# The opening of a two-block transformer kernel put in a set order, worked by token halves

## The chip, the cores and the metric

The kernel runs on one core of a Trainium2 chip. Times are microseconds (us) of device time for the whole kernel, the median of the runs. The engines: TensorE (PE in the profile; its weight loads are PEld), VectorE (DVE), ScalarE (ACT), GpSimd (POOL) and SyncE (SP), which here only issues DMAs. Each works through its instructions in one fixed order and waits at the first whose inputs or buffers are not ready.

## The reference, cut to what matters

Two transformer blocks of two layers each, 512 tokens, width 1024, float32. Only the beginning is touched by the change: a layer norm without weights, a scale and a shift from a conditioning vector (adaLN), and the first columns of a projection.

```python
def first_block(x, c, w_in, ...):
    c_act = jax.nn.silu(c)
    h = layer_norm(x)                      # mean and variance over 1024 features, per token
    for l in range(DEPTH):
        ada = (c_act @ w_ada[l] + b_ada[l])[:, None, :]
        sh1, sc1, g1, sh2, sc2, g2 = jnp.split(ada, 6, axis=-1)
        u = h * (1.0 + sc1) + sh1
        y = mixer(u, w_in[l], ...)         # z = u @ w_in, then mLSTM heads, attention, gates
        h = layer_norm(DN_ALPHA * h + g1 * y, ...)
        ...
```

The second block needs `softplus(-lam)` of a vector of 512 (here `softplus_cols`), long after the opening.

## The kernel before, in words

Activations lie transposed: features on the 128 partitions, 512 tokens along the free dimension, so x is 8 tiles of 128 x 512 (`self.x`, k from 0 to 7, called inputs below). A product multiplies a 128 x 128 block of weights with such a tile. For accuracy each operand is split into a rounded high part and a remainder (`h`/`l` of an activation, `wh`/`wl` of a weight), and a product is three matmuls: wh by h, wh by l, wl by h. All weights come as one stream (`block`): SP loads chunks of 16 blocks (1 MB, two buffers), and a unit of 8 blocks is cast on ACT (`wh`, L589) and its remainder taken on VectorE (`wl`, L592) when its first block is wanted; there are 5 buffers for units, so a cast can wait until products have released one.

The opening is `setup` and the first half of `first_block`. `setup` issues the loads (SP and ACT share them): the vectors, the constants for sums, x whole, the other constants; it makes silu of c, softplus (`softplus_cols`, a Tanh and an Exp of one table set on ACT, 27 small instructions on VectorE), and scales columns of the vectors. Then the norm: `Mean.half` sums over features by matmuls with ones into a PSUM bank; `spread` copies the sums to SBUF and spreads them with one more matmul; `mean` subtracts and squares; `scale` takes the reciprocal root and corrects it in three steps (`rstd`); `plain` multiplies (five tiles on VectorE, three on GpSimd). For every input k, `ada_tile` loads four tiles of adaLN weights (1 MB in all), sums them against silu(c) on TensorE (L820), copies the sums (L824) and turns them to columns (L827, L829); the output u of input k is formed from these columns (L1360 to L1362), GpSimd scales the residual (L1364), and five products follow (L1367 to L1369): the gates and four tiles of head 0's queries and keys, in five PSUM banks.

Behind it `mlstm_gates` takes the gates' accumulator through ACT and VectorE (L884 to L905, three table loads among them and around), and TensorE meanwhile works at the values of head 0 (`proj_tokens`, L625 to L629) until it needs the transposed gates (L911). The order of all this on each engine is made by a scheduler from the program's text and its dependencies, unless `behind` ties two instructions.

Later norms already work by token halves: `mean`, `squares`, `scale` and `out` take a half (`hs`), and `proj_halves` forms the products of the first 256 tokens of several accumulators, then of the second; `residual` then rescales the tile itself. The lines the prediction uses from there are L238 (sums), L248 (spread), L347 (copy of the mean), L349, L352 (subtract, square), L855 (reciprocal root), L377 to L379 (output), L649 to L653 (products).

Of the kernel before, what the change touches and what calls it, by code (L numbers as in the profile page):

```python
# [16 lines left out]
P = 128  # L17
# [209 lines left out]
class Mean:  # L227
# [16 lines left out]
    def spread(self, tmp, hs):  # L244
        m, nc = self.m, self.m.nc
        nc.scalar.copy(tmp.f[:, hs], self.rows[:, hs])
# [31 lines left out]
class Norm:  # L278
# [3 lines left out]
    def __init__(self, m, r, kind, cols, res=None):  # L282
        self.m, self.r, self.kind, self.cols, self.res = m, r, kind, cols, res
        self.sum = None
# [4 lines left out]
    def start(self, total):  # L289
        if self.sum is None:  # L290
            self.sum = Total(self.m) if total else Mean(self.m, self.m.pso, "o")
# [47 lines left out]
    def mean(self, hs):  # L339

        m, nc, r = self.m, self.m.nc, self.r
        if self.kind != "ln":
            return
        if hs.start == 0:
            self.sq = Mean(m, m.pss, "s")
        mu = self.sum.spread(self.tmp, hs)
        nc.scalar.copy(self.y.f[:, hs], mu[:, hs])  # L347
        for k in range(KD):
            nc.vector.tensor_tensor(out=r[k].f[:, hs], in0=r[k].f[:, hs], in1=self.y.f[:, hs], op=ALU.subtract)  # L349
        self.sqs = [m.get() for _ in range(KD)]  # L350
        for k in range(KD):
# [10 lines left out]
    def scale(self, hs):  # L362
# [3 lines left out]
        if self.kind == "ln":  # L366
            var, eps = self.sq.spread(self.a, hs), LN_EPS
# [4 lines left out]
    def out(self, k, hs):  # L372
# [5 lines left out]
        nc.scalar.activation(h.r[:, hs], t, AF.Identity, bias=sh, scale=1.0)  # L378
# [10 lines left out]
    def plain(self, hs):  # L389

        self.mean(hs)
        self.squares(hs, 0)
        self.squares(hs, 1)
        self.scale(hs)
        for k in range(KD):
            eng = self.m.nc.gpsimd if k in (2, 5, 7) else self.m.nc.vector
            eng.tensor_tensor(out=self.r[k].f[:, hs], in0=self.r[k].f[:, hs], in1=self.y.f[:, hs], op=ALU.mult)
        self.done()

    def done(self):  # L400
        m = self.m
        if self.kind == "ln" and self.cols is not None:
# [121 lines left out]
class Model:  # L524
    def __init__(self, ctx, tc, ins, out, dbg=None, stop=None):
# [20 lines left out]
        self.later = []  # L546

# [29 lines left out]

    def block(self, name, l, k, c):
# [3 lines left out]
        if n % CHUNK == 0:  # L582
            self.wt = self.wtp.tile([P, CHUNK * P], F32, name="wt")
            nc.sync.dma_start(out=self.wt, in_=self.ins["ws"][n // CHUNK].rearrange("p a b -> p (a b)"))
        if n % UNIT == 0:
# [3 lines left out]
            copy = nc.scalar.copy(self.wh, src)  # L589
            if n == 0:  # L590
                self.behind(copy, self.last_rsqrt)
# [40 lines left out]
    def proj_halves(self, specs, xs, k0=0, by_input=False):  # L632
# [9 lines left out]
        blks = {}  # L642
# [35 lines left out]

    def split(self, src, pair):
# [20 lines left out]
    def setup(self):  # L700
        nc = self.nc
        self.vecs = self.cp.tile([P, NVEC], F32, name="vecs")
        nc.sync.dma_start(out=self.vecs, in_=self.ins["vecs"])
# [7 lines left out]
        nc.scalar.dma_start(out=self.consts, in_=self.ins["cst"][:, n:])  # L711
# [10 lines left out]
        nc.vector.tensor_copy(self.ident_r, self.ident)  # L722
        self.csil = self.cp.tile([P, 16], F32, name="csil")
        c = self.vec("c1", 0, 16)
        th = self.small(16, "th_c")
        nc.scalar.activation(th, c, AF.Tanh, scale=0.5)
        nc.vector.tensor_scalar(out=th, in0=th, scalar1=0.5, scalar2=0.5, op0=ALU.mult, op1=ALU.add)
        nc.vector.tensor_mul(self.csil, th, c)
        self.n2sp = self.softplus_cols()
        self.n4sp = self.cp.tile([P, 4], F32, name="n4sp")  # L730
        nc.vector.tensor_scalar(out=self.n4sp, in0=self.n2sp, scalar1=2.0, scalar2=None, op0=ALU.mult)
# [12 lines left out]
        nc.vector.tensor_scalar(out=v, in0=v, scalar1=1.0, scalar2=None, op0=ALU.add)  # L744
# [1087 lines left out]
```

## Time and profile before

| | |
|---|---|
| runs | 3477.12, 3477.94, 3479.91 us; median 3477.94 |
| the profiled execution | 3481.36 us, its span 3479.6 us |
| mean granted clock of TensorE over the span | 0.993 of full speed |
| TensorE busy | 98% of the span |
| VectorE, ScalarE, GpSimd busy | 62%, 42%, 5% |
| DMA | 395.72 MB, mean 114 GB/s |

Times in the profile count from the start of the span. A busy TensorE is not one at its peak, since matmuls are pipelined and their ends are modelled; the spacing of two starts says more than one duration. A matmul of plain float32 (sums, spreads, columns) shows as two instructions in the profile, one of the rounded operands (products) as one.

### The profile page before, as it was taken

Reading aid. Unit: us, or ns where it says so; the run is one execution under the profiler, and the core shown is the slowest. Engines: PE = TensorE matmul, PEld = TensorE weight load, DVE = VectorE, ACT = ScalarE, POOL = GpSimd, SP = SyncE. Lnnn points to the kernel's source line nnn. Section 1 sums busy time; section 2 is a strip of 40 time slices with the busy share of each in tenths; the row PEclk is TensorE's granted clock in tenths of the full one; section 3 lists DMA queues with packets and bytes.
Section 4 is the critical chain, followed back from the end, with each engine's and each line's share of the span. In section 5 each row is a group of like instructions: output and inputs, shape, how many; then the busy total and the mean of one; then the engine's idle time right before and its main releaser. Section 6 shows DMA issues by size and latency. Waiting matters only on the chain.

```text
span 3479.6 us, 45264 instructions
## 1 busy us (share of the span) xinstructions
PE 3405.2 (98%) x17783; PEld 2787.9 (80%) x17783; DVE 2159.5 (62%) x4071; ACT 1450.8 (42%) x2536; POOL 183.8 (5%) x252
## 2 busy tenths in 40 slices
PE   7999999999999999999999999989999999999999
PEld 5788777778888888877788888877688888888887
DVE  5875545648663687554534856378888555875353
ACT  4543555225222454355523422237753234753231
POOL 1110010010000011001100000001000000000000
PEclk9999999999999999999999999999999999999999
DMA  5222223634552222222222555221146432122222
GB/s 218 91 75 84 75 78 105 223 121 176 205 188 97 73 91 79 80 84 73 79 97 85 200 187 194 94 71 61 37 145 232 163 114 85 50 74 97 97 97 73
DMA packets 76117, 395.72 MB, mean 114 GB/s; under 512 B 9200, under 2 KB 10480, under 8 KB 42496
## 3 DMA queue, kind: packets, MB, share of 16 engines
q1 hardware_dynamic: 69408, 377.90, 30.5%
q0 software_dynamic: 4480, 12.69, 1.2%
q8 instruction: 140, 2.29, 0.3%
q10 hardware_dynamic: 2016, 2.25, 0.2%
q14 instruction: 73, 0.60, 0.1%
HBM read 390.60 MB, written 2.20 MB: 113 GB/s over the span
## 4 chain that ended last, share of the span: by engine, by line
PE 85%; DVE 7%; ACT 2%; DMA 2%; issue 1%; POOL 0%; DVEq 0%; ACTq 0%; POOLq 0%
PE acc L604 22%; PE acc L606 21%; PE acc L605 21%; PE acc L649 2%; PE acc L652 2%; PE acc L653 2%; DMA wada<-in_ada_dram 1%; PE o L1168 1%; PE o L1583 1%; DVE wl L592 1%; PE s L1132 1%; DVE slot L778 1%; PE acc L625 1%; PE acc L629 1%; PE acc L628 1%
## 5 line engine op out<-in xcount | busy, mean ns | idle before, releaser
L604 PE MATMUL acc<-slot,wh 128*128 128x512 f32 x3461 | 1375.7, 398 | 14.0 <-DVE slot L874 9.3
L605 PE MATMUL acc<-slot,wh 128*128 128x512 f32 x3461 | 1364.0, 394 | 0.0
L606 PE MATMUL acc<-slot,wl 128*128 128x512 f32 x3461 | 1363.3, 394 | 0.0
L589 ACT CAST wh<-wt 128x1024 fp32r<-128x1024 f32 x522 | 547.2, 1049 | 1230.0 <-PE acc L605 1021.9
L592 DVE TENSOR_TENSOR wl<-wt,wh 128x1024 fp32r<-128x1024 f32 x522 | 647.7, 1242 | 526.1 <-ACT wh L589 521.3
L604 PEld LDWEIGHTS acc<-slot,wh 128*128 128x128 f32 x3461 | 652.7, 189 | 164.2 <-ACT wh L589 13.9
L606 PEld LDWEIGHTS acc<-slot,wl 128*128 128x128 f32 x3461 | 652.1, 188 | 146.6 <-issue 4.9
L605 PEld LDWEIGHTS acc<-slot,wh 128*128 128x128 f32 x3461 | 652.9, 189 | 140.8 <-issue 5.4
L778 DVE SCALAR_TENSOR_TENSOR slot<-wada,csil,slot 128x512 f32<-128x512 f32 x308 | 232.1, 754 | 63.2 <-DMA wada<-in_ada_dram 57.6
L649 PE MATMUL acc<-slot,wh 128*128 128x256 f32 x726 | 206.9, 287 | 6.2 <-ACT slot L512 5.9
L652 PE MATMUL acc<-slot,wh 128*128 128x256 f32 x726 | 205.6, 283 | 0.0
L653 PE MATMUL acc<-slot,wl 128*128 128x256 f32 x726 | 204.3, 282 | 0.1
L680 ACT CAST slot<-slot 128x512 fp32r<-128x512 f32 x204 | 125.3, 620 | 168.9 <-DVE slot L1332 47.2
L1266 DVE SCALAR_TENSOR_TENSOR slot<-acc,ada,slot 128x512 f32<-128x512 f32 (+1 forms) x109 | 70.2, 647 | 160.8 <-PE acc L606 120.8
L874 DVE SCALAR_TENSOR_TENSOR slot<-acc,vecs,slot 128x510 f32<-128x510 f32 (+2 forms) x217 | 159.9, 746 | 7.8 <-ACT slot L869 5.2
L681 DVE TENSOR_TENSOR slot<-slot,slot 128x512 fp32r<-128x512 f32 x204 | 144.4, 714 | 30.8 <-ACT slot L680 21.3
L649 PEld LDWEIGHTS acc<-slot,wh 128*128 128x128 f32 x726 | 136.8, 189 | 13.4 <-ACT slot L512 6.5
L652 PEld LDWEIGHTS acc<-slot,wh 128*128 128x128 f32 x726 | 137.3, 189 | 2.5 <-issue 1.2
L653 PEld LDWEIGHTS acc<-slot,wl 128*128 128x128 f32 x726 | 137.4, 189 | 0.7 <-DVE wl L592 0.3
L625 PE MATMUL acc<-wh,slot 128*128 128x256 f32 x288 | 81.5, 283 | 0.0
L628 PE MATMUL acc<-wh,slot 128*128 128x256 f32 x288 | 81.4, 283 | 0.0
L629 PE MATMUL acc<-wl,slot 128*128 128x256 f32 x288 | 80.9, 281 | 0.0
(391 smaller groups left out, 3939.6 us busy)
## 6 DMA issues: line engine op xcount, KB each, us to landing
wt<-in_ws_dram SPq DMA_DIRECT2D x261, 1024.0 KB, 4.8
wada<-in_ada_dram SPq DMA_DIRECT2D x176, 512.0 KB, 4.4
slot<-in_ada_dram SPq DMA_DIRECT2D x32, 256.0 KB, 6.1
slot<-drc POOLq DMA_DIRECT2D x16, 256.0 KB, 3.5
slot<-in_bias_dram POOLq DMA_DIRECT2D x16, 256.0 KB, 3.0
slot<-dr POOLq DMA_DIRECT2D x32, 128.0 KB, 3.0
out_dram<-slot SPq DMA_DIRECT2D x8, 256.0 KB, 2.0
slot<-in_xT_dram SPq DMA_DIRECT2D x4, 256.0 KB, 5.4
```

The lines of the kernel that those rows point to most:

```text
L589: copy = nc.scalar.copy(self.wh, src)
L592: nc.vector.tensor_tensor(out=self.wl, in0=src, in1=self.wh, op=ALU.subtract)
L604: nc.tensor.matmul(acc, wh, xs[k].h.r, start=k == 0, stop=False)
L605: nc.tensor.matmul(acc, wh, xs[k].l.r, start=False, stop=False)
L606: nc.tensor.matmul(acc, wl, xs[k].h.r, start=False, stop=k == n - 1)
L649: m = nc.tensor.matmul(acc[:, hs], wh, xs[k].h.r[:, hs], start=k == 0, stop=False)
L652: nc.tensor.matmul(acc[:, hs], wh, xs[k].l.r[:, hs], start=False, stop=False)
L653: last[a] = nc.tensor.matmul(acc[:, hs], wl, xs[k].h.r[:, hs], start=False, stop=k == n - 1)
L680: copy = self.nc.scalar.copy(pair.h.r, src)
L681: self.nc.vector.tensor_tensor(out=pair.l.r, in0=src, in1=pair.h.f, op=ALU.subtract)
L778: nc.vector.scalar_tensor_tensor(out=acc.f, in0=wt[:, j, :], scalar=c, in1=acc.f, op0=ALU.mult, op1=ALU.add)
L874: nc.vector.scalar_tensor_tensor(out=out[:, lo:hi], in0=acc[:, lo + d:hi + d], scalar=w, in1=out[:, lo:hi], op0=ALU.mult, op1=ALU.add)
```

## The change

- x comes in token halves: first halves on SP and ACT, then the vectors, the first weight chunk and adaLN tile 0, then the second halves. The 16 columns of c and c_2 have a small load of their own ahead; the other constants come after the opening.
- The norm works by halves with the functions of the later norms, its first sums and its squares in one PSUM bank. `out` forms u from the centred x, the reciprocal root and the columns, so the five and three multiplications of `plain` go; the residual (alpha times the root times x) becomes eight VectorE instructions that can run later, and GpSimd's eight go.
- The products go through `proj_halves`: all five accumulators for the first 256 tokens, input by input, then again for the second. Between the products of an input stand, in this order, the next tile's sums and columns, the next output, the weights of the input after it, and a piece of the second half's norm (`other`). AdaLN tiles are loaded three ahead.
- `in_order` ties PE, DVE and ACT instructions of `first_norm` to the order of the text; instructions outside it can still be put between them by the scheduler.
- Softplus moves into `mixer`, behind the gates in the text and not ahead of the last output on ACT (`last_out`).

```diff
 class Mean:
...
+    def collect(self, tmp, hs):
+        self.m.nc.scalar.copy(tmp.f[:, hs], self.rows[:, hs])
...
 class Norm:
...
+    def means(self, hs, mu):
+        m = self.m
+        if self.sq is None:
+            self.sq = Mean(m, m.pss, "s")
+        m.nc.scalar.copy(self.y.f[:, hs], mu[:, hs])
+        self.sqs = {}
...
+    def centre(self, hs, ks):
...
-        for k in range(KD):
+        for k in ks:
             nc.vector.tensor_tensor(out=r[k].f[:, hs], in0=r[k].f[:, hs], in1=self.y.f[:, hs], op=ALU.subtract)
...
+        for k in ks:
             nc.scalar.activation(self.sqs[k].f[:, hs], r[k].f[:, hs], AF.Square)
...
-            if n == 0:
-                self.behind(copy, self.last_rsqrt)
...
+    def in_order(self):
+        traced = self.nc.cur_bb.bb.instructions
+        n = len(traced)
+        yield
+        last = {}
+        for i in list(traced[n:]):
+            if i.engine in (mybir.EngineType.PE, mybir.EngineType.DVE, mybir.EngineType.Activation):
+                if i.engine in last:
+                    self.tc.add_manual_dep(i, last[i.engine].name, mybir.DependencyInfo(
+                        mybir.DependencyClass.NoSync, mybir.DependencyReason.DATA), reason="order of the text")
+                last[i.engine] = i
...
-        for k in range(KD):
-            (nc.sync if k % 2 else nc.scalar).dma_start(out=self.x[k].f, in_=self.ins["xT"][k])
+        for hs in HALVES:
+            for k in range(KD):
+                (nc.sync if k % 2 or hs.start else nc.scalar).dma_start(out=self.x[k].f[:, hs], in_=self.ins["xT"][k][:, hs])
+            if hs.start == 0:
+                self.vecs = self.cp.tile([P, NVEC], F32, name="vecs")
+                nc.sync.dma_start(out=self.vecs, in_=self.ins["vecs"])
+                self.chunk(0)
+                self.adas = deque([self.ada_load(0)])
...
     def mixer(self, l, u):
         nc = self.nc
         gates = self.mlstm_gates(l, u)
+        if l == 0:
+            self.n2sp = self.softplus_cols()
...
-        norm = Norm(self, r, "ln", None)
-        for k in range(KD):
-            norm.half(k, slice(0, T))
-        self.behind(self.load_rsqrt(r[5].f[:, 0:1]), self.sp_exp)
-        norm.plain(slice(0, T))
...
-        for k in range(KD):
-            self.ada_tile(k)
...
+        with self.in_order():
+            norm = self.first_norm(r, A(0, 1), A(0, 0))
+        self.setup_late()
...
+    def first_norm(self, r, sc, sh):
...
+        norm = Norm(self, r, "ln", (sc, sh))
+        self.load_rsqrt(self.eps[:, 0:1])
+        norm.sq = Mean(self, self.pss, "s")
+        norm.start(False, norm.sq)
+        for k in range(KD):
+            norm.half(k, first)
+        self.setup_columns()
+        norm.mean(first)
+        weights(0)
+        norm.squares(first, 0)
+        norm.squares(first, 1)
+        norm.scale(first)
+        self.adas += [self.ada_load(1), self.ada_load(2)]
+        self.chunk(1)
+        self.ada_columns(0, self.ada_sums())
+        norm.out(0, first)
+        weights(1)
+        ahead = self.proj_halves(specs, norm.u, by_input=True, blks=blks)
...
+        def other(k):
+            if k == 1:
+                for j in range(KD):
+                    norm.half(j, second)
+                norm.sum.collect(norm.tmp, second)
+            elif k == 2:
+                norm.means(second, norm.sum.spread(norm.tmp, second, True))
+            elif k in (3, 4):
+                norm.centre(second, range(4 * k - 12, 4 * k - 8))
+            elif k == 5:
+                norm.squares(second, 0)
+                norm.squares(second, 1)
+                norm.sq.collect(norm.a, second)
+            elif k == 6:
+                norm.scale(second, True)
+
+        for k in range(KD):
+            if k + 3 < KD:
+                self.adas.append(self.ada_load(k + 3))
+            if k == 3:
+                self.chunk(2)
+            rs = self.ada_sums() if k + 1 < KD else None
+            products(range(2))
+            if rs is not None:
+                self.ada_columns(k + 1, rs)
+                norm.out(k + 1, first)
+            weights(k + 2)
+            products(range(2, 5))
+            other(k)
+        norm.out(0, second)
+        for k in range(KD):
+            if k + 1 < KD:
+                norm.out(k + 1, second)
+            products()
...
-        self.sp_exp = nc.scalar.activation(e, t, AF.Exp, scale=-1.0)
+        self.behind(nc.scalar.activation(t, lam, AF.Abs), self.last_out)
+        nc.scalar.activation(e, t, AF.Exp, scale=-1.0)
```

What the orders show, at three places. First TensorE at the first products. In these rows `s` is the bank of adaLN sums, `t` that of the columns, `acc` and `o` the five accumulators. Before (L820 sums, L827 columns, L1367 to L1369 products):

```order
L820 MATMUL s<-slot_424,csil 32x256 x2
L1367 MATMUL acc<-slot_256,wh 128x512 x3
L1367 MATMUL o<-slot_256,wh 128x512 x2
L827 MATMUL t<-dup,slot_385 128x1 x2
L1368 MATMUL acc<-slot_257,wh 128x512
L1369 MATMUL acc<-slot_256,wl 128x512
```

Now (L855 sums, L867 columns, L653 to L657 products; slot_246 to slot_249 are the weights of tile 1):

```order
L867 MATMUL t<-dup,slot_273 128x1 x2
L855 MATMUL s<-slot_246,csil 32x256 x2
L855 MATMUL s<-slot_247,csil 32x256 x2
L855 MATMUL s<-slot_248,csil 32x256 x2
L855 MATMUL s<-slot_249,csil 32x256 x2
L653 MATMUL acc<-slot_223,wh 128x256
L656 MATMUL acc<-slot_224,wh 128x256
L657 MATMUL acc<-slot_223,wl 128x256
L653 MATMUL acc<-slot_223,wh 128x256
L656 MATMUL acc<-slot_224,wh 128x256
L657 MATMUL acc<-slot_223,wl 128x256
L867 MATMUL t<-dup,slot_304 128x1 x2
```

The next tile's sums now stand ahead of an input's products, and its columns behind the second of the five accumulators; the matmuls are of 256 tokens.

Second, ACT around inputs 5 and 6 of the first half (L859 copies a tile's sums, L389 forms the output's high part, L595 casts a weight unit, L363 squares the second half). Before, ACT's row there held only these (L824, L1360, L589):

```order
L824 COPY slot_524<-s 128x256
L1360 ACTIVATE slot_264<-slot_95,ada_171 128x512
L824 COPY slot_567<-s 128x256
L1360 ACTIVATE slot_266<-slot_96,ada_171 128x512
L1360 ACTIVATE slot_268<-slot_97,ada_171 128x512
```

Now:

```order
L389 ACTIVATE slot_233<-slot_523,ada_144 128x256
L595 CAST wh<-wt 128x1024
L363 ACTIVATE slot_544<-slot_95 128x256
L363 ACTIVATE slot_545<-slot_96 128x256
L363 ACTIVATE slot_546<-slot_97 128x256
L363 ACTIVATE slot_547<-slot_98 128x256
L859 COPY slot_561<-s 128x256
L389 ACTIVATE slot_235<-slot_573,ada_144 128x256
```

The copy of tile 6's sums now stands behind a weight cast and four squares; the squares need subtractions which on VectorE stand behind that cast's remainder.

Third, ACT at the end of the opening. Before:

```order
L1360 ACTIVATE slot_270<-slot_98,ada_171 128x512
L884 ACTIVATE slot_642<-acc,vecs 64x512
L885 ACTIVATE slot_643<-acc,vecs 64x512
L869 ACTIVATE slot_680<-acc,vecs 128x512
L886 ACTIVATE slot_644<-slot_643 64x512
L869 ACTIVATE slot_693<-acc,vecs 128x512
L887 ACT_TABLE_LOAD
```

Now (L924 is the former L884, L1628 and L1629 are softplus):

```order
L389 ACTIVATE slot_237<-slot_768,ada_144 128x256
L1628 ACTIVATE sp_838<-vecs 128x4
L595 CAST wh<-wt 128x1024
L1629 ACT_TABLE_LOAD
L1629 ACTIVATE sp_839<-sp_838 128x4
L924 ACTIVATE slot_804<-acc,vecs 64x512
```

A cast of later weights, softplus' table load and its exponential now stand ahead of the gates; the load for the gates' exponential (L887 before) is gone.

## Rows read from the trace of the kernel before

**Rows 1.** The page, part 4: the chain that ended last, by engine.
```profile
PE 85%; DVE 7%; ACT 2%; DMA 2%; issue 1%; POOL 0%; DVEq 0%; ACTq 0%; POOLq 0%
```

**Rows 2.** Stretches: us, PE, PEld, DVE, ACT, POOL busy, granted clock, DMA share, GB/s.
```profile
2.50:6.00 3.50, 0.00 (x0) 0.03 (x1) 1.27 (x14) 0.00 (x0) 0.00 (x0) 1.00 0.98 366
6.00:14.00 8.00, 6.70 (x18) 1.05 (x18) 1.86 (x13) 3.91 (x8) 0.00 (x0) 1.00 1.06 402
14.00:21.00 7.00, 4.92 (x24) 2.58 (x24) 6.73 (x25) 2.86 (x5) 0.00 (x0) 0.54 1.03 390
...
35.00:42.00 7.00, 4.56 (x13) 3.81 (x14) 6.97 (x11) 3.52 (x4) 2.66 (x3) 0.51 0.13 26
42.00:72.50 30.50, 28.94 (x177) 21.46 (x175) 15.33 (x23) 10.21 (x15) 5.47 (x5) 1.00 0.52 202
72.50:76.00 3.50, 3.36 (x8) 2.69 (x9) 0.69 (x1) 0.48 (x2) 1.12 (x1) 0.51 0.01 2
...
86.00:89.50 3.50, 0.86 (x8) 0.80 (x9) 3.46 (x6) 2.40 (x5) 0.00 (x0) 1.00 0.00 0
```

**Rows 3.** Timeline of PE: start, duration, line, xcount [idle before <-releaser].
```profile
33.20 0.97 PE L1367 MATMUL acc<-slot,wh 128*128 128x512 f32 x3 [2.41 <-ACT slot L1360]
...
77.49 0.39 PE L1369 MATMUL o<-slot,wl 128*128 128x512 f32 x1
...
88.64 0.46 PE L911 MATMUL t<-consts,slot 64*128 64x64 f32 x4 [2.91 <-DVE slot L898]
```

**Rows 4.** The page, part 6: DMA issues of x on SP, KB each, us to landing.
```profile
slot<-in_xT_dram SPq DMA_DIRECT2D x4, 256.0 KB, 5.4
```

**Rows 5.** Timeline of ACT and DVE in a later norm's second half.
```profile
801.94 0.37 ACT L347 COPY slot<-t 128x256 f32<-128x256 f32 x1
...
803.02 2.61 ACT L352 ACTIVATE slot<-slot 128x256 f32<-128x256 f32 x8
...
809.38 0.47 ACT L855 ACTIVATE slot<-t,eps 128x256 f32<-128x256 f32 x1 [0.79 <-PE t L248]
813.39 1.31 ACT L378 ACTIVATE slot<-slot,cols 128x256 fp32r<-128x256 f32 x3 [3.54 <-DVE slot L377]
...
802.35 2.78 DVE L349 TENSOR_TENSOR slot<-slot,slot 128x256 f32<-128x256 f32 x8
...
812.88 1.27 DVE L377 SCALAR_TENSOR_TENSOR slot<-slot,cols,slot 128x256 f32<-128x256 f32 x3
```

**Rows 6.** Timeline of PE: columns and sums of adaLN, sums, spread, half-width products.
```profile
49.18 0.50 PE L827 MATMUL t<-dup,slot 128*128 128x1 f32 x4
49.61 1.48 PE L820 MATMUL s<-slot,csil 128*32 128x256 f32 x18
...
805.25 0.64 PE L238 MATMUL s<-slot,sums 128*32 128x256 f32 x8
...
808.64 0.70 PE L248 MATMUL t<-slot,sums 128*128 128x256 f32 x2
...
820.01 0.28 PE L649 MATMUL acc<-slot,wh 128*128 128x256 f32 x1
820.13 0.28 PE L652 MATMUL acc<-slot,wh 128*128 128x256 f32 x1
```

**Rows 7.** The page, part 5: weight casts and their remainders, busy, mean ns.
```profile
L589 ACT CAST wh<-wt 128x1024 fp32r<-128x1024 f32 x522 | 547.2, 1049 | 1230.0 <-PE acc L605 1021.9
L592 DVE TENSOR_TENSOR wl<-wt,wh 128x1024 fp32r<-128x1024 f32 x522 | 647.7, 1242 | 526.1 <-ACT wh L589 521.3
```

**Rows 8.** Timeline of ACT at the gates: first instruction, and the table load.
```profile
75.61 0.68 ACT L884 ACTIVATE slot<-acc,vecs 64x512 f32<-64x512 f32 x1 [3.02 <-PE acc L1369]
...
78.99 1.28 ACT L887 ACT_TABLE_LOAD   x1
```

**Rows 9.** Timeline of DVE: one of softplus' small instructions between two large ones.
```profile
15.28 0.16 DVE L1534 TENSOR_SCALAR sp<-sp 128x4 f32<-128x4 f32 x1
15.35 0.68 DVE L349 TENSOR_TENSOR slot<-slot,slot 128x512 f32<-128x512 f32 x1
```

More of the change, by code (lines that the diff above doesn't have):

```diff
@@ L2 @@
 from collections import deque
[L3 removed]
+from contextlib import ExitStack, contextmanager
 import numpy as np
@@ L242, in half, with spread @@
         self.last[g] = mm
-    def spread(self, tmp, hs):
+    def collect(self, tmp, hs):
+        self.m.nc.scalar.copy(tmp.f[:, hs], self.rows[:, hs])
+    def spread(self, tmp, hs, collected=False):
         m, nc = self.m, self.m.nc
-        nc.scalar.copy(tmp.f[:, hs], self.rows[:, hs])
+        if not collected:
+            self.collect(tmp, hs)
         b = m.pst.tile([P, T], F32, name="t")
@@ L339, in mean @@
     def mean(self, hs):
-        m, nc, r = self.m, self.m.nc, self.r
[L342 to L347, printed above, removed]
-        for k in range(KD):
+        if self.kind == "ln":
+            self.means(hs, self.sum.spread(self.tmp, hs))
+            self.centre(hs, range(KD))
+    def means(self, hs, mu):
[5 more added lines that the diff above has]
+    def centre(self, hs, ks):
+        m, nc, r = self.m, self.m.nc, self.r
+        for k in ks:
             nc.vector.tensor_tensor(out=r[k].f[:, hs], in0=r[k].f[:, hs], in1=self.y.f[:, hs], op=ALU.subtract)
-        self.sqs = [m.get() for _ in range(KD)]
-        for k in range(KD):
+        for k in ks:
+            self.sqs[k] = m.get()
+        for k in ks:
             nc.scalar.activation(self.sqs[k].f[:, hs], r[k].f[:, hs], AF.Square)
@@ L387, in residual @@
         nc.scalar.activation(r, r, AF.Identity, bias=b[:, k:k + 1], scale=1.0)
[L389 to L394, printed above, removed]
-        for k in range(KD):
-            eng = self.m.nc.gpsimd if k in (2, 5, 7) else self.m.nc.vector
-            eng.tensor_tensor(out=self.r[k].f[:, hs], in0=self.r[k].f[:, hs], in1=self.y.f[:, hs], op=ALU.mult)
-        self.done()
     def done(self):
         m = self.m
-        if self.kind == "ln" and self.cols is not None:
+        if self.res is not None and self.cols is not None:
             m.later += [lambda k=k: self.residual(k) for k in range(KD)]
@@ L575, in dbg, with chunk @@
             raise StopIteration
+    def chunk(self, n):
+        self.wt_next = self.wtp.tile([P, CHUNK * P], F32, name="wt")
+        self.nc.sync.dma_start(out=self.wt_next, in_=self.ins["ws"][n].rearrange("p a b -> p (a b)"))
     def block(self, name, l, k, c):
@@ L1395, in first_block, with weights, products, residual @@
         return r, last["n"]
+    def first_norm(self, r, sc, sh):
+        nc = self.nc
+        first, second = HALVES
+        specs = [("w_in", 0, c) for c in ("gates", 0, P, 8 * P, 9 * P)]
+        blks = {}
+        def weights(k):
+            for a, sp in enumerate(specs):
+                if k < KD:
+                    blks[a, k] = self.block(*sp[:2], k, sp[2])
+        norm = Norm(self, r, "ln", (sc, sh))
[16 more added lines that the diff above has]
+        ahead = self.proj_halves(specs, norm.u, by_input=True, blks=blks)
+        def products(tiles=range(len(specs))):
+            for a in tiles:
+                sp = specs[a]
+                _, _, done, acc = next(ahead)
+                if done:
+                    self.ready[sp] = acc
+        def other(k):
[31 more added lines that the diff above has]
+            products()
+        norm.done()
+        def residual(k):
+            nc.vector.scalar_tensor_tensor(out=r[k].f, in0=r[k].f, scalar=ALPHA, in1=norm.y.f, op0=ALU.mult, op1=ALU.mult)
+        self.later += [lambda k=k: residual(k) for k in range(KD)]
+        return norm
```

86 lines of the change are left out of this document (40 added, 46 removed).

## The prediction

> **What bounds the kernel now.** I read the chain of waits first: 85% of it is TensorE [rows 1], so over most of the span only fewer or faster matmuls would help, and the change leaves these alone. The exception is the opening, read next in stretches and as a timeline. There the reader is to see three things. DMA is full from 2.5 us on (366, then 402 GB/s) and nearly empty by 35 to 42 us [rows 2]. The first product starts at 33.20 us, the last at 77.49, and TensorE then meets a wait of 2.91 us for the gates, which ends at 88.64 [rows 3]. And the granted clock is near half (1.2 of 2.4 GHz) in 14 to 21, 35 to 42 and 72.5 to 76 us, each time after a stretch in which TensorE stood idle in part. What the change can win is how much earlier than 77.7 us (77.49 and 0.23 for the last product) the 40 blocks are through, less what the gates behind them then lose. Outside this the two programs' orders agree but for buffer numbers and two swapped neighbours, so I carry the difference at 88.64 us to the end unchanged.
>
> **The first norm, by halves.** Before, the norm waited for all of x (2 MB) behind the vectors. Now it needs 1.05 MB of first halves and 0.15 MB of constants: at the rate of [rows 2] 3.1 us after 2.5, so 5.6. One unknown is what the 128 KB pieces cost; before, 256 KB took 5.4 us from issue to landing while queued [rows 4]. If halves moved at full rate x is there at 5.5, at half the rate at 8.2; I take 6.0, near the first, since the queues are filled side by side and the rate of [rows 2] was already held with several transfers in flight. The Trainium skill, "DMA: Bandwidth & Descriptors", speaks against the halves: its rule (section Bandwidth) is to batch to 1 MiB or more, and its fit (section Anatomy of one DMA) of 2.0 us plus bytes over 436 GB/s gives an estimated 2.3 us for 128 KB; were the four of a queue to run one behind the other, x would be there near 11.7 us.
>
> The chain then has half-width steps, whose durations I take from a later norm that already works by halves. Sums of eight 1.3 at most, of which 0.3 follow the last transfer; copy 0.37, spread 0.70, copy 0.37 [rows 5, 6]. Eight subtractions 2.78, the last square 0.41 behind them [rows 5]. One weight cast of 1.05 now stands on ACT between the squares and the next copy [rows 7]. Copy 0.37, spread 0.70, reciprocal root 0.47, three dependent corrections at 0.48 [rows 5, 6]. With 0.05 for each hand-over this is 9.4 us: the norm is ready at 15.4. The scaling of the constant columns on VectorE hides beside the sums.
>
> **First products.** Tile 0's adaLN sums are 16 instructions at 1.48/18 = 0.08 us, so 1.3 us, its columns 0.43 to 0.50 [rows 6], then a product of scale on VectorE 0.48 and a cast on ACT 0.5 [rows 5]. Because PE's order puts tile 1's sums ahead of the first product, and because TensorE has been nearly idle, I take the clock to be near half here, as it was at 14 to 21 us before. Tile 1's sums start at 17.5 us, the first product near 20, against 33.2.
>
> **Work from 17.5 us to the end of the first half.** At full clock: seven sums 9.1 (7 x 1.3); seven columns 3.1 (0.45 each); 120 matmuls of 256 columns at the spacing of 0.12 (820.01 to 820.13, [rows 6]) 14.4; and the second half's norm, put between products, 2 x 1.3 of sums and 2 x 0.70 of spreads, 4.0. Together 30.6. The loads keep ahead of that: up to tile 7 they are 14 MB in all, at 0.39 MB/us from 2.5 us on [rows 2] the last lands near 39, and is wanted after 44.
>
> Waits. The set order puts four subtractions and four squares ahead of tile 6's copy on ACT, and they stand behind a weight cast and its remainder. From input 5's cast to input 6's: 1.05 + 1.22 [rows 7] + 1.4 + 0.41 + 0.37 + 0.45 + 0.16 + 0.48 + 0.5 = 6.0, against 3.5 us of TensorE's work (five products 1.8, sums 1.3, columns 0.45). That is a new wait of 2.5 us; a smaller one at input 5, where four subtractions stand without a weight cast, 0.8. Clock: I charge 3.5 us, for one stretch near half at the start and one after the 2.5 us wait, each costing half of 3.5 us [rows 2]. End of the first half: 17.5 + 30.6 + 3.3 + 3.5 = 54.9.
>
> **The second half.** From the reciprocal root to the first product 1.3 us remain uncovered by the last products. The 120 matmuls take 14.4. In front of three inputs the casts of later weight units (1.05, then 1.22, then the low part 0.48: 2.75 us [rows 5, 7]), which wait for a buffer, exceed the products that cover them by about 0.9 each: 2.6. The eight residual products, moved from GpSimd to VectorE at the price of a full-width one, about 0.7, fill waits for ACT and add nothing as long as an input takes TensorE 1.8 us. Sum 18.3; the last product ends at **73.2 instead of 77.7**, 4.5 us earlier.
>
> **The gates behind it.** Before, ACT took up the gates at 75.61, 2.1 us ahead of the end, because they are the first of five accumulators [rows 8]. Now they are done 1.4 us ahead, and ACT comes later still: a cast waiting for a buffer, the table load of 1.28 and softplus' exponential stand first, to 0.3 us before the end. That is 1.8 us lost; 1.28 come back, since the same load is no longer inside the gates (78.99, [rows 8]). Softplus' VectorE instructions interleave: one between two large ones costs 0.07 (15.28 to 15.35, [rows 9]), and 8 of 27 lie where VectorE has no slack (3.46 of 3.50 us busy [rows 2]): 0.6. Together 1.1 us back.
>
> **Sum.** 4.5 - 1.1 = 3.4 us faster. Against the profiled execution's 3481.36 that is 3478.0; that execution stands 3.4 above the median of the runs, 3477.94, from which I take it: **3474.5 us**.
>
> **The rivals.**
> 1. *The set order runs without its waits.* If TensorE holds the full clock from the first product and the wait at input 6 is covered, 3.5 + 3.3 are not paid: 10.2 us faster, 3467.7. For it: TensorE held the full clock through 42 to 72 us with gaps below half a us. Against it: the chain of 6.0 us is in the printed order. 0.24.
> 2. *The gates take the gain.* If softplus' chain runs at 0.2 per dependent step rather than 0.07, and the weights' remainders come late, VectorE loses 2.5 more: 0.9 us gained, 3477. For it: VectorE is full there [rows 2]. Against it: the scheduler set them alternately. 0.17.
> 3. *The halves of x transfer slowly.* At half the rate the norm is 2.2 us later, and with it everything to the end of the opening: 1.2 gained, 3476.7. By the fit of the Trainium skill's page named above it would be 5.7 later, and the kernel 2.3 slower, 3480.2. 0.13, since [rows 2] show transfers running side by side.
> 4. *The clock stays near half through the first half*, the case on the other side. Its place is the stretch from 20 to 55 us, its price one us for each us of full-speed work. It eats the gain from 3.4 us of such work beyond the 3.5 already charged, and ends over 7 us slower beyond 10.4. Were all 30.6 us done at half clock, with the waits of 3.3 then covered, 30.6 - 3.5 - 3.3 = 23.8 would be lost and 3.4 gained: the kernel at 3498. For it: bursts of sums, columns and products wait on each other, and each idle stretch of [rows 2, 3] cost the clock. Against it: at half speed TensorE is the late one and so is busy all the time, as in 38 to 42 us before, after which the clock came back. The Trainium skill, "TensorE: Matmul & The Clock Gate", HAM oscillation, says the same of bursts between waits: throttled anew each time; the stretches of [rows 2] agree. 0.08.
>
> **How the numbers follow.** The forecast has 0.38, with its own range from 3470.5 to 3479 (clock 0 to 7 us, x at 5.5 to 7). Measurement of this kernel can tell about 0.2%, 7 us, from no change. Faster by more: rival 1 nearly whole and the low end of the forecast, 0.31. Slower by more: rival 4 and the far end of rival 3, 0.09. Within: 0.60. The range from 3466 to 3482 leaves out rival 4, the low part of rival 1 and little of the rest, under 0.2.
>
> **What would show it.** Right: x's first sums by 6 us and the norm's corrections done near 15.5; the first product at 19 to 21; one wait of 2 to 3 us before tile 6's columns; the last product at 71 to 75; a wait for the gates of 3 to 4 us, ended near 85. Wrong: a clock near half after 25 us in more than one stretch; the sums of a tile waiting for DMA after tile 2; or a gates' wait longer than 5 us. A last product before 69 us would mean that the waits I charged are not there.

## The result, and the profile after

The changed kernel takes **3523.1 us** (median of 4 runs, 3522.54 to 3526.63); the kernel before, run beside it, 3477.53. The ratio is 1.0132, 95% interval 1.0115 to 1.015: 45.6 us slower, where 3.4 us faster was forecast and the range ended at 3482. Its profiled execution has a span of 3521.0 us.

Where the time lies is read from the clock first, then from a stretch far behind the opening. The mean granted clock is 0.995, no lower than the 0.993 before, and TensorE is busy 98% of the span, as before. The windows of TensorE in two stretches of the kernel before (columns: stretch, its length, busy time and instructions, granted clock, DMA share, GB/s):

```profile
600.00:700.00 100.00, 96.46 (x419) 1.00 0.64 228
3200.00:3400.00 200.00, 200.00 (x876) 1.00 0.27 99
```

The same windows of the changed kernel:

```profile
600.00:700.00 100.00, 99.28 (x423) 0.99 0.63 216
3200.00:3400.00 200.00, 200.00 (x862) 1.00 0.27 95
```

In 3200 to 3400 us both kernels do nothing but 512-column products, without a gap, at the full clock of 2.4 GHz, and the changed one does 862 where the other does 876. So each product costs 1.6% more, far from anything that was moved. The page's costliest groups, before:

```profile
L604 PE MATMUL acc<-slot,wh 128*128 128x512 f32 x3461 | 1375.7, 398 | 14.0 <-DVE slot L874 9.3
L605 PE MATMUL acc<-slot,wh 128*128 128x512 f32 x3461 | 1364.0, 394 | 0.0
L606 PE MATMUL acc<-slot,wl 128*128 128x512 f32 x3461 | 1363.3, 394 | 0.0
```

and after, with the weight steps that answer to [rows 7]:

```profile
L608 PE MATMUL acc<-slot,wh 128*128 128x512 f32 x3461 | 1383.9, 400 | 15.2 <-DVE slot L914 11.1
L609 PE MATMUL acc<-slot,wh 128*128 128x512 f32 x3461 | 1376.8, 398 | 0.0
L610 PE MATMUL acc<-slot,wl 128*128 128x512 f32 x3461 | 1375.0, 397 | 0.0
L595 ACT CAST wh<-wt 128x1024 fp32r<-128x1024 f32 x522 | 547.2, 1049 | 1286.2 <-PE acc L609 1060.3
L596 DVE TENSOR_TENSOR wl<-wt,wh 128x1024 fp32r<-128x1024 f32 x522 | 645.2, 1237 | 544.2 <-ACT wh L595 539.1
```

Same counts, same idle time before them; ScalarE and VectorE take what they took. Only the products are longer. Between starts (all pairs of neighbours of one width that start less than 300 ns apart, worked out from the trace) 512-column matmuls stand 232.5 ns apart instead of 228.9, 256-column ones 123.9 instead of 121.8. The 256-column mean also holds some 250 gaps near 210 ns, most of them at matmuls that are not products, so only its differences count here. 10,145 x 3.6 ns + 4,207 x 2.1 ns = 36.5 + 8.8 = 45.3 us, against a loss of 45.6. In 600 to 700 us TensorE waits less than before, but the two windows do not hold the same work, and over the whole span it is idle for 71.9 us instead of 74.4 (72.3 in run e3 below, whose products are the fastest): that a part of the loss is hidden in waits is not shown.

Two lines of the diff, neither an instruction of the opening, stand behind this. The columns of c got a 64 byte tile of their own among the constants, and the tile `th_c` one buffer instead of four:

```diff
+        cols = self.cp.tile([P, 16], F32, name="c_cols")
-        th = self.small(16, "th_c")
+        th = self.small(16, "th_c", 1)
```

SBUF is handed out in the order constants, wt, wh and wl, wada, small tiles, slots. One buffer of `th_c` is 64 bytes. So the weights moved 64 bytes up, and the slots 64 up and 192 down: 128 bytes down (in the two programs the first wh lies at byte 51072, now 51136; slot 0 at 106432, now 106304). Buffers of wh and wl are 4096 bytes, slots 2048, a block of weights 512, so in every product the distance from its weights to its slot is the same modulo 256: 64 bytes before, 128 after.

The opening itself, in the timeline of TensorE after (start, time, instructions, idle before and what ended it):

```profile
21.64 0.39 PE L653 MATMUL acc<-slot,wh 128*128 128x256 f32 x1
46.22 1.00 PE L867 MATMUL t<-dup,slot 128*128 128x1 f32 x4 [3.06 <-ACT slot L859]
76.07 0.28 PE L657 MATMUL o<-slot,wl 128*128 128x256 f32 x1
77.42 0.39 PE L629 MATMUL acc<-wh,slot 128*128 128x256 f32 x1 [1.07 <-ACT slot L925]
87.79 0.46 PE L951 MATMUL t<-consts,slot 64*128 64x64 f32 x4 [1.33 <-DVE slot L938]
92.67 0.46 PE L951 MATMUL t<-consts,slot 64*128 64x64 f32 x4 [0.67 <-ACT slot L945]
95.20 0.80 PE L608 MATMUL acc<-slot,wh 128*128 128x512 f32 x1 [2.07 <-DVE slot L914]
```

Against [rows 3] the first product is 11.6 us earlier, the last 1.4, the gates' transposes (L951, before L911 at 88.64) 0.9. Then a wait of 2.07 us that was not there before stands ahead of the first 512-column product, which began at 93.82 before: the changed opening is by then 1.4 us behind. (One trace is one execution, and differences of this size are not safe; see the part on the prediction.) The windows of these stretches, after:

```profile
42.00:46.00 4.00, 1.17 (x14) 1.00 1.02 421
46.00:50.00 4.00, 3.78 (x21) 0.53 0.39 158
50.00:54.00 4.00, 4.00 (x37) 0.61 0.00 1
96.00:104.00 8.00, 8.00 (x26) 0.69 0.08 16
```

### The profile page after: what moved, and what is told of

Its sections match the earlier page's. It is cut to its first block, busy times and chain, and to the rows that moved or that the text cites. A ratio compares the mean times of both kernels' runs of the same rounds, so it can differ in the third digit from the quotient of the medians.

```text
span 3521.0 us, 45620 instructions
## 1 busy us (share of the span) xinstructions
PE 3449.1 (98%) x17939; PEld 2804.2 (80%) x17939; DVE 2162.3 (61%) x4101; ACT 1454.0 (41%) x2556; POOL 170.4 (5%) x241
## 4 chain that ended last, share of the span: by engine, by line
PE 87%; DVE 5%; ACT 2%; DMA 1%; issue 1%; POOL 0%; DVEq 0%; ACTq 0%; POOLq 0%
PE acc L608 22%; PE acc L609 22%; PE acc L610 22%; PE acc L653 2%; PE acc L656 2%; PE acc L657 2%; PE o L1208 1%; PE o L1688 1%; PE s L1172 1%; PE acc L633 1%; PE acc L629 1%; PE acc L632 1%; PE o L1212 1%; PE s L1571 1%; DVE wl L596 1%
## 5 line engine op out<-in xcount | busy, mean ns | idle before, releaser
L608 PE MATMUL acc<-slot,wh 128*128 128x512 f32 x3461 | 1383.9, 400 | 15.2 <-DVE slot L914 11.1
L595 ACT CAST wh<-wt 128x1024 fp32r<-128x1024 f32 x522 | 547.2, 1049 | 1286.2 <-PE acc L609 1060.3
L608 PEld LDWEIGHTS acc<-slot,wh 128*128 128x128 f32 x3461 | 654.2, 189 | 179.4 <-ACT wh L595 13.7
L610 PEld LDWEIGHTS acc<-slot,wl 128*128 128x128 f32 x3461 | 653.4, 189 | 154.0 <-issue 4.6
L609 PEld LDWEIGHTS acc<-slot,wh 128*128 128x128 f32 x3461 | 654.0, 189 | 152.2 <-issue 5.1
L653 PE MATMUL acc<-slot,wh 128*128 128x256 f32 x774 | 223.5, 290 | 7.0 <-ACT slot L512 5.8
L656 PE MATMUL acc<-slot,wh 128*128 128x256 f32 x774 | 221.7, 287 | 1.7 <-DVE slot L390 1.5
L657 PE MATMUL acc<-slot,wl 128*128 128x256 f32 x774 | 220.2, 285 | 0.0
L698 ACT CAST slot<-slot 128x512 fp32r<-128x512 f32 x204 | 125.4, 620 | 154.5 <-POOL slot L1290 45.6
L653 PEld LDWEIGHTS acc<-slot,wh 128*128 128x128 f32 x774 | 146.3, 190 | 17.9 <-issue 8.2
L656 PEld LDWEIGHTS acc<-slot,wh 128*128 128x128 f32 x774 | 146.6, 189 | 5.3 <-DVE slot L390 2.9
L657 PEld LDWEIGHTS acc<-slot,wl 128*128 128x128 f32 x774 | 146.8, 190 | 0.6 <-DVE wl L596 0.3
L629 PE MATMUL acc<-wh,slot 128*128 128x256 f32 x288 | 82.0, 285 | 1.8 <-ACT slot L925 1.1
```

The source lines that it names most:

```text
L608: nc.tensor.matmul(acc, wh, xs[k].h.r, start=k == 0, stop=False)
L609: nc.tensor.matmul(acc, wh, xs[k].l.r, start=False, stop=False)
L610: nc.tensor.matmul(acc, wl, xs[k].h.r, start=False, stop=k == n - 1)
L653: m = nc.tensor.matmul(acc[:, hs], wh, xs[k].h.r[:, hs], start=k == 0, stop=False)
L656: nc.tensor.matmul(acc[:, hs], wh, xs[k].l.r[:, hs], start=False, stop=False)
L657: last[a] = nc.tensor.matmul(acc[:, hs], wl, xs[k].h.r[:, hs], start=False, stop=k == n - 1)
```

## Experiments

P: the place of weights and slots sets the pace. O: the order does. All runs on the kernel before keep the order of all five engines (one or two short GpSimd memsets of the padding aside). Everything in one table, distance being the slots' address less that of the weights, modulo 256 bytes, "gap" the mean between starts as above. Each run's ratio is to runs of the kernel before on the same chip; e1 to e14 were run on four chips:

```
run                distance       gap 512, 256 (ns)  median us  ratio to before [95%]
before             64             228.9  121.8
after              128            232.5  123.9       3523.1     1.0132 [1.0115, 1.0150]
e1  after          64             228.9  121.7       3478.9     1.0004 [0.9995, 1.0012]
e2  before         128            232.6  123.3       3518.4     1.0115 [1.0101, 1.0128]
e3  before         0              227.1  124.4       3469.1     0.9975 [0.9963, 0.9987]
e4  before         192            233.1  120.7       3519.2     1.0118 [1.0104, 1.0132]
e5  before         0              227.2  124.4       3469.3     0.9974 [0.9963, 0.9985]
e6  after          0              227.1  124.7       3471.0     0.9973 [0.9963, 0.9983]
e7  before         32             233.1  122.0       3518.1     1.0108 [1.0086, 1.0130]
e8  before         224 (-32)      233.1  123.0       3518.6     1.0107 [1.0087, 1.0128]
e9  before         128            232.6  123.1       3517.7     1.0100 [1.0081, 1.0119]
e10 before         192            233.1  121.6       3516.4     1.0094 [1.0075, 1.0113]
e11 before         256, so 0      227.1  124.1       3472.6     0.9972 [0.9961, 0.9983]
e12 after, softplus late  0       227.1  124.5       3470.2     0.9964 [0.9954, 0.9975]
e13 before         wh 0, wl 128   231.1  123.4       3501.6     1.0062 [1.0041, 1.0082]
e14 before         wh 128, wl 0   233.1  123.8       3523.3     1.0125 [1.0103, 1.0147]
```

**Place or order: e1 to e4.** e1, on the changed kernel:

```diff
-        cols = self.cp.tile([P, 16], F32, name="c_cols")
+        cols = self.small(16, "c_cols", 1)
-        th = self.small(16, "th_c", 1)
+        th = self.small(16, "th_c", 3)
```

> The changed kernel with its three weight rings, the wada ring and the 60 slots put back, byte for byte, on the SBUF places that they have in the kernel before: the 64 byte tile c_cols goes from the constants to the small tiles, and th_c gets 3 buffers. The order of all engines is that of the changed kernel. Theory P (place): the change's 45.6 us are the pace of the products, 512-column matmuls that start 232.5 ns apart instead of 228.9 and 256-column ones 123.9 instead of 121.8, and the pace hangs on where weights or slots lie. Then the starts are 228.9 ns apart again and the time falls by some 45 us to 3474 to 3480, and what is left against the kernel before is the opening's own effect, forecast at -3.4 us. Rival O (order): the new order, with another rotation of slots and weight buffers, sets the pace; then 232.5 ns and 3523 us stay.

e2, on the kernel before (e3: `th_c` with 3; e4: `th_c` with 2 and no padding):

```diff
-        self.vecs = self.cp.tile([P, NVEC], F32, name="vecs")
+        pad = self.cp.tile([P, 16], F32, name="pad"); nc.gpsimd.memset(pad[:, 0:1], 0.0); self.vecs = self.cp.tile([P, NVEC], F32, name="vecs")
-        th = self.small(16, "th_c")
+        th = self.small(16, "th_c", 1)
```

> The kernel before with the places of the changed one: a 64 byte tile that nothing reads ahead of the constants (weight rings and wada 64 bytes up) and th_c with one buffer (slots 128 bytes down); same order on all engines. Theory P: starts of 512-column products 232.5 ns apart and 3523 us (3518 to 3528). Rival O: 228.9 ns and 3477.5 us.

> The kernel before with the weight rings (wt, wh, wl) and wada alone 64 bytes up; the slots stay where they were. Theory PW (the weights' place decides): 232.5 ns and some 3523 us. Rival PS (the slots' place decides): 228.9 ns and 3477.5 us. If the distance between the two decides, neither: some other pace.

> The kernel before with the 60 slots alone 128 bytes down (th_c with 2 buffers); the weight rings stay. Theory PW (the weights' place decides): 228.9 ns and 3477.5 us. Rival PS (the slots' place decides): 232.5 ns and some 3523 us.

P holds, both ways. The changed order on the old places has the old pace and the old time; the old order on the new places has the new pace and nearly all of the loss (38 us against the runs beside it; its interval overlaps that of the changed kernel). The page's rows of e1:

```profile
L608 PE MATMUL acc<-slot,wh 128*128 128x512 f32 x3461 | 1377.4, 398 | 16.1 <-DVE slot L914 11.3
L609 PE MATMUL acc<-slot,wh 128*128 128x512 f32 x3461 | 1363.3, 394 | 0.0
```

and of e2:

```profile
L604 PE MATMUL acc<-slot,wh 128*128 128x512 f32 x3461 | 1380.9, 399 | 13.8 <-DVE slot L874 9.5
L605 PE MATMUL acc<-slot,wh 128*128 128x512 f32 x3461 | 1375.0, 397 | 0.0
```

e1 also gives what the change was meant for: +0.04%, -0.05 to +0.12%, so -1.7 to +4.2 us. e3 and e4 together then fit neither theory: e4 comes out as PS has it, but in e3 moving the weights alone changes the pace too, for the better. That leaves the distance between the two. The page's rows of e3:

```profile
L604 PE MATMUL acc<-slot,wh 128*128 128x512 f32 x3461 | 1364.5, 394 | 13.3 <-DVE slot L874 9.1
L605 PE MATMUL acc<-slot,wh 128*128 128x512 f32 x3461 | 1357.5, 392 | 0.0
```

and of e4:

```profile
L604 PE MATMUL acc<-slot,wh 128*128 128x512 f32 x3461 | 1384.0, 400 | 16.6 <-DVE slot L874 9.4
L605 PE MATMUL acc<-slot,wh 128*128 128x512 f32 x3461 | 1377.8, 398 | 0.0
```

**Distance or the slots' own place: e5 to e8.** e5, on the kernel before:

```diff
-        self.csil = self.cp.tile([P, 16], F32, name="csil")
+        self.csil = self.small(16, "csil", 1)
-        th = self.small(16, "th_c")
+        th = self.small(16, "th_c", 2)
```

> The kernel before, order unchanged, with the weight rings 64 and the slots 128 bytes down (csil goes from the constants to the small tiles, th_c gets 2 buffers). Counted modulo 512, weights then start at 320 and slots at 320: the distance from weights to slots is 0, as in the run e3 (448 and 448, 227.1 ns), while the slots have the place of the two slow runs (320: 232.5 and 233.1 ns). Theory D (the distance between a product's weights and its slot decides; so far 0, 64, 384, 448 gave 227.1, 228.9, 232.5, 233.1 ns): 227.1 ns and some 3469 us. Rival S (the slots' own place decides): 232 to 234 ns and some 3520 us.

e6 is the changed kernel with one number altered:

```diff
-        th = self.small(16, "th_c", 1)
+        th = self.small(16, "th_c", 3)
```

> The changed kernel with th_c at 3 buffers instead of 1 and nothing else: the slots go back to where they were before, the weights stay 64 bytes up, so both start at 448 modulo 512, as in the run e3. Theories D and S agree here: starts of 512-column products 227.1 ns apart, and, as the order itself was worth nothing in the run e1 (+1.4 us, -1.8 to +4.2), a time like that of e3: 3466 to 3472 us, some 52 us below the changed kernel and 8 to 10 below the one before. If the gain of e3 hung on the old order, 3478 us.

e7, with the padding of e2 (e8: also `th_c` with 3):

```diff
-            col = self.small(4, "vcol")
+            col = self.small(4, "vcol", 3)
```

> The kernel before with weights at 448 as in e3 and the slots 32 bytes up (480 modulo 512): distance 32. Theory D: between the runs with distance 0 (227.1 ns, 3469 us) and 64 (228.9 ns, 3480 us), some 228 ns. If blocks of 64 bytes count (each 2048 byte column run then begins in the middle of one), slower than both: over 229 ns, over 3480 us.

> The kernel before with weights at 448 as in e3 and the slots 32 bytes down (416 modulo 512): distance -32. Theory D, if the pace jumps between -64 (448: 233.1 ns) and 0 (227.1 ns): either 227 or 233 ns, which of them says on which side of the jump it lies; if it goes evenly, 230 ns and some 3490 us. If blocks of 64 bytes count, like e7: over 229 ns.

The distance decides: e5 has the slots where e2 and e4 had them and is as fast as e3. e6 takes some 50 us off the changed kernel, and is 0.27% faster than the kernel before; e5, with the order of before at the same distance, is 0.26% faster, so the new order is worth nothing measurable at this pace either. 32 bytes to either side of 0 are slow; for e7 it was the second of the outcomes named, for e8 the slow side of the jump.

**How far the pattern goes: e9 to e11.** e9 has the `csil` line of e5 alone; e10 and e11 also move the first two (four) columns of softplus to the small tiles:

```diff
-        t, e, y, y2, s = (self.cp.tile([P, 4], F32, name=f"sp{k}") for k in range(5))
+        t, e, y, y2, s = (self.small(4, f"sp{k}", 1) if k < 2 else self.cp.tile([P, 4], F32, name=f"sp{k}") for k in range(5))
```

> The kernel before, order unchanged, csil moved from the constants to the small tiles: the weight rings go 64 bytes down (320 modulo 512), the slots stay (448): distance 128. Of the distances tried, 0 and 64 are fast (227.1 and 228.9 ns), 32, -32, -64 and -128 slow (232.5 to 233.1 ns). Theory D1 (a distance of 0 or more, in whole steps of 64 bytes, is fast): 227 to 229.5 ns, 3468 to 3484 us. Theory D2 (64 is already the edge, and the pace gets slower with every step away from 0): 230.5 to 233 ns, 3495 to 3523 us.

> The kernel before, order unchanged, csil and two columns of softplus moved to the small tiles: weight rings at 256, slots at 448 modulo 512, distance 192. Theory D1: 227 to 229.5 ns, 3468 to 3484 us. Theory D2: 232 to 233 ns, some 3518 to 3523 us.

> The kernel before, order unchanged, csil and four columns of softplus moved to the small tiles: weight rings at 192, slots at 448 modulo 512, distance 256. If the pattern repeats every 256 bytes, this is distance 0: 227.1 ns and 3469 us. If it repeats every 512: 232 to 233 ns and some 3520 us.

D2 holds as far as 192, and e11 shows a repeat after 256 bytes. -128 and +128 (e2, e9), -64 and +192 (e4, e10) agree to 0.1 ns in the 512-column gap. For 256 columns the order of the distances is another one: 192 is best there (120.7 and 121.6), 0 worst.

**Which weights: e13 and e14.** e13 is e2 with a gap behind wh, e14 is e5 with the same gap:

```diff
+            if n == 0: gap = self.whp.tile([P, 32], F32, name="gap", bufs=1); nc.gpsimd.memset(gap[:, 0:1], 0.0)
             self.wl = self.whp.tile([P, UNIT * P], F32R, name="wl")
```

> The kernel before, order unchanged, with wh at distance 0 from the slots and wl, behind a gap of 128 bytes, at distance 128 (modulo 256). Theory L (what collides is the load of the next product's weights with the column run of the product under way): the starts are 232 to 233 ns apart only from the second to the third matmul of a block (hi by lo weights follow: wl is loaded meanwhile), 227 ns in the other two gaps, 229 ns on the mean, and the time lies a third of the way from 3469 to 3518: 3482 to 3489 us. Rival W (a product's own weights count, not the next one's): the slow gap is the one from the third matmul to the next first. Rival T (another tile that moved with the weights, wt or wada, or the small tiles, sets the pace): all three gaps alike.

> The reverse: wh at distance 128 from the slots, wl at distance 0. Theory L: the gap from the second to the third matmul is 227 ns, the other two 232 to 233, mean 231, time 3499 to 3506 us. Rival W: the gap from the third matmul to the next first is the fast one. Rival T: all three alike.

Mean gaps inside a block, from some 3,100 pairs each: first matmul to second (wh, wh), second to third (wh, wl), third to the next first (wl, wh):

```
        wh->wh  wh->wl  wl->wh
e13     227.3   232.4   233.9 ns
e14     232.6   232.6   234.8 ns
```

The page's rows of e13 (L605 and L606 are wh, L607 is wl):

```profile
L607 PE MATMUL acc<-slot,wl 128*128 128x512 f32 x3461 | 1378.5, 398 | 0.0
L606 PE MATMUL acc<-slot,wh 128*128 128x512 f32 x3461 | 1377.9, 398 | 0.0
L605 PE MATMUL acc<-slot,wh 128*128 128x512 f32 x3461 | 1363.4, 394 | 13.3 <-DVE slot L875 9.0
```

Rival T falls, since in e13 the gap between two wh products stays at the fast pace while wt, wada and the small tiles are the same for all three. L and W fall too, each as put: a gap was fast only where the weights under way and the next ones both lay at distance 0. So it is the places of wh and wl themselves, those of both neighbours; the times (3501.6 and 3523.3) lie above what L gave. Why the gap behind wl is the longest in both runs is open.

**The gates: e12.** e6, with softplus moved in `mixer` from behind the gates into the loop over the eight output products:

```diff
-        if l == 0:
-            self.n2sp = self.softplus_cols()
...
-            nc.scalar.activation(th.f, acc, AF.Tanh, scale=0.5)
+            self.last_out = nc.scalar.activation(th.f, acc, AF.Tanh, scale=0.5)
+            if l == 0 and m == 2:
+                self.n2sp = self.softplus_cols()
...
```

> The run e6 (changed kernel, distance 0) with the softplus columns taken out of the gates and computed some 300 us later, in the third of the eight output products of layer 0, long before their first reader at over 2000 us. Theory G (the changed opening gives its gain back in the gates, where 20 short VectorE steps and a table load of 1.28 us of softplus hold the ScalarE and VectorE steps that free the product banks: TensorE waited 0.81 and 2.07 us at 92.25 and 94.78 us and then ran at half clock to some 101 us): the ninth 512-column product of L608, at 103.1 us in the run e1 (99.9 in the kernel before), starts at 98 to 100 us, and the time falls by 2 to 4 us against e6 (3471.0), to 3467 to 3469. Rival: the wait at the gates comes from the order of the convolutions alone; then the mark stays at 102 to 103.5 us and the time within 1.5 us of e6.

TensorE's waits between 85 and 100 us in e12:

```profile
85.17 0.46 PE L951 MATMUL t<-consts,slot 64*128 64x64 f32 x4 [2.46 <-DVE slot L938]
90.03 0.46 PE L951 MATMUL t<-consts,slot 64*128 64x64 f32 x4 [0.88 <-ACT slot L945]
98.06 0.80 PE L608 MATMUL acc<-slot,wh 128*128 128x512 f32 x1 [2.57 <-ACT slot L1056]
```

and in e6:

```profile
85.30 0.46 PE L951 MATMUL t<-consts,slot 64*128 64x64 f32 x4 [1.33 <-DVE slot L938]
90.19 0.46 PE L951 MATMUL t<-consts,slot 64*128 64x64 f32 x4 [0.64 <-ACT slot L945]
92.71 0.50 PE L608 MATMUL acc<-slot,wh 128*128 128x512 f32 x1 [2.07 <-DVE slot L914]
```

The ninth L608 starts at 98.06, inside theory G's bounds; but those were set from e1, and in e6, with softplus in its old place, it starts at 99.94, inside them too, so the mark decides nothing. The time, 3470.2, is the rival's. The reason given falls as well: without softplus the gates end 0.13 us earlier, no more. The scheduler only put the products differently, a wait of 2.57 us follows, and at the 25th L608 e12 (125.06) is 0.4 us behind e6 (124.62). The ratios, 0.9964 and 0.9973, have overlapping intervals: a gain of softplus' later place is not shown. e12 has the lowest ratio, 0.36% (0.25 to 0.46%) below the kernel before, but its interval overlaps those of all runs at distance 0, which accounts for most of it.

## Why the prediction was wrong

**The step that failed** is in its first part: "Outside this the two programs' orders agree but for buffer numbers and two swapped neighbours, so I carry the difference at 88.64 us to the end unchanged." The orders did agree. But the same order is not the same pace: the buffers lay elsewhere, and some 14,350 gaps grew by 2 to 4 ns on the mean, 45.3 us in all. The forecast has no term for the tile `c_cols` and the buffers of `th_c`, that is, it put them at nothing without a reason, and no rival had the buffers' places in it. e1 and e2 show both halves of it.

The rest can be judged point by point, by the changed kernel and by e6, in which the 512-column pace is fast. One caution holds for all of it: the traces are single executions, and the opening differs from one to the next. e3, e5 and e11 have the same order and pace, yet the 33rd 512-column product of the projections (L604) starts at 134.40, 132.57 and 131.60 us; the granted clock of 14 to 21 us, 0.54 in [rows 2], is 0.76 in e3 and e5 and 1.00 in e11. What lies within two to three us between two traces shows no effect of the order.

- *x by halves, norm ready at 15.4.* x's sums began at 4.2 us but their spread only at 8.4, where 6.7 was forecast: of the two ends for x, 5.5 and 8.2, the truth lay nearer to the far one, that of rival 3. A 128 KB piece took 3.7 us (median) from issue to landing. The 11.7 us of rival 3 did not come, since the sums of all first halves were through by 7.9; the fit behind it (the Trainium skill, "DMA: Bandwidth & Descriptors", Anatomy of one DMA) is given there for DMAs issued by GpSimd, and these were issued by SP and ACT. Then the scaling of the constant columns, costed at nothing because it "hides beside the sums", did not hide: the vectors landed at 9.6, and VectorE, in the set order, began the subtractions behind the scaling, at 10.79, while the mean they need was copied by 10.06. The corrections ended at 18.2. VectorE after:

```profile
9.61 0.71 DVE L759 TENSOR_SCALAR vecs<-vecs 128x96 f32<-128x96 f32 x6 [4.21 <-DMA vecs<-in_vecs_dram]
10.79 2.77 DVE L359 TENSOR_TENSOR slot<-slot,slot 128x256 f32<-128x256 f32 x8
...
17.75 0.43 DVE L898 SCALAR_TENSOR_TENSOR slot<-slot,slot 128x256 f32<-128x256 f32 x1
```

- *First product near 20.* 21.6; 22.0 in e6. Tile 0's sums and columns were ready beside the late norm, which took back a part of the delay.
- *A new wait of 2.5 us at tile 6's copy.* 3.06, at the place named, ended by that copy. About half a us of it is not the chain that was forecast: the cast ahead of the squares waited for its weights, so the loads did not quite "keep ahead". In e1 and e6, where that cast waits for no DMA, the wait is 2.55 and 2.50. The cast in the changed kernel:

```profile
41.78 1.05 ACT L595 CAST wh<-wt 128x1024 fp32r<-128x1024 f32 x1 [0.45 <-DMA wt<-in_ws_dram]
```

- *Clock, 3.5 us in two stretches.* No stretch at the start of the products (1.00 in 14 to 21 us); one behind the wait, at about half from 46 to 53 us, which costs those 3.5. In e6 there are two, as forecast: 14 to 21 us has a clock of 0.86, and behind the wait the window 50 to 54 us is at full clock already:

```profile
46.00:50.00 4.00, 4.00 (x37) 0.57 0.30 121
50.00:54.00 4.00, 3.89 (x37) 1.00 0.00 0
```

- *Last product at 73.2.* It starts at 76.1, at 75.6 in e1, at 73.6 in e6. The pace isn't why e6 is ahead, its 256-column gap being the longest of the three (124.7 ns); its half-clock stretch behind the wait is shorter. Why is open, and such stretches differ between executions, as said above. With the order of before at e6's distance the last product starts at 78.2, 77.8 and 76.3 (e3, e5, e11), so the opening itself did gain 2.7 to 4.6 us up to here, where 4.5 was forecast.
- *Gates ended near 85.* 87.8, 87.4 in e1, 85.3 in e6. Of the wait of 3 to 4 us 1.07 stood ahead of the products of head 0's values (L629) and 1.33 at L951.
- *From there unchanged to the end.* Wrong here as well, on a small scale: the 2.07 us ahead of L608, and in e1 the half clock behind it from 94 to past 100 us, took the rest (in the changed kernel 0.69 in 96 to 104 us, so that "a clock near half after 25 us in more than one stretch", named as a sign of being wrong, did come). At the 33rd L608 e1 is 0.3 us behind the kernel before, and e6, at 132.05, lies among e3, e5 and e11: nothing of the gain is to be seen there. The times agree: e1 gave -1.7 to +4.2 us where -3.4 was forecast. Rival 2 (the gates take the gain) named the place nearly, but not the mechanism: by e12 it isn't softplus. What decides these waits is not settled.

Taken by itself the new order falls in the case "within 0.2%", which had 0.60.

## What to carry to other kernels

A diff that adds or drops a tile, however small, moves every buffer allocated behind it: compare the SBUF places of weights and moving operands, not only the orders, and if the spacing of equal matmuls changes at full granted clock in a stretch that the change doesn't touch, look there first. A kernel that lives on back-to-back products can try a few paddings between its weight rings and its data: here moves of 32 to 128 bytes were worth between -0.3% and +1.3% of the whole time, and the best distance differed by product width.

## What was not expected of the hardware

The pace of a 512-column product with reloaded weights (rounded float32; other types were not tried) depends on the distance from its weights to the moving operand modulo 256 bytes: 227.1 ns at 0, 228.9 at 64, 232.5 to 233.1 at 32, 128, 192 and 224. The weight loads themselves take what they took (PEld of L604 before and L608 after: 189 ns). It isn't other engines' traffic: in the gaps in which no VectorE, ScalarE or GpSimd instruction ran and no DMA packet was under way (some 1,200 in each trace, after 300 us) the means are 228.9 before and 232.7 after. The Trainium skill, "SBUF — State Buffer", Terms, says that DMA and engine accesses to SBUF cannot conflict; the traces agree, with 228.95 ns under DMA and 228.82 without, before. No run came to the 216 ns that the Trainium skill, "TensorE: Matmul & The Clock Gate", Step-by-step, states as the back-to-back gap of 512-column matmuls; the least here, with a weight load for each, is 227.1. What in the reading of weights and moving operand makes the distance count is open; that it counts was shown by runs whose orders are the same and whose buffers alone moved.
